# Down projections: loads of borrowed tiles and stored sums issued by GpSimd's queue instead of SyncE's

## The chip, the cores and the metric

The kernel runs on one core of one Trainium2 chip. The metric is the device time of one execution in microseconds (us). The engines are named as in the profile: PE (TensorE, with PEld for its weight loads), DVE (VectorE), ACT (ScalarE), POOL (GpSimd) and SP (SyncE). SPq and POOLq are the instruction queues of SP and POOL, which here issue DMA transfers.

## What is computed

A decoder trunk of two layers over 256 tokens of width 2048, all in float32. The part that the change touches is the gated feed-forward block at the end of each layer:

```python
def conv_ffn(h, w_up, cw, cb, w_down):
    S = h.shape[1]
    a = h @ w_up
    ap = jnp.pad(a, ((0, 0), (CONV_W - 1, 0), (0, 0)))
    c = sum(ap[:, k:k + S] * cw[k] for k in range(CONV_W)) + cb
    gate, val = c[..., :D_FF], c[..., D_FF:]
    return (jax.nn.silu(gate) * val) @ w_down
```

`w_up` is 2048 x 11264 and `w_down` 5632 x 2048 in each layer. The rest (token mixing, attention over memory and over the sequence, norms) is unchanged.

## The kernel before

Every float32 weight is split on the chip into a high and a low part of a reduced format (ACT writes the high part `whi`, DVE the low part `wlo`), and PE makes three products for each float32 product. The raw weights stream from memory into tiles named `raw`, of which there are four; `whi` has four tiles and `wlo` five.

`ffn` cuts the hidden width into three parts of 4, 4 and 3 groups of 512 columns (`FF_GROUPS`). For each part it makes the up projection of all groups (through `gemm_fm`), and then two down phases (`down_phase`, called with `col` 0 and 1024), one for each half of the 2048 output columns. A down phase goes over 8 (or 6) pairs of 128-row blocks of `w_down`, in an order written out in `FF_FAST`. A pair has two rows of blocks, each 128 x 1024 (512 KB).

- A pair that is not "fast" is split as it is (`plain_pair`) and takes 24 matmuls.
- A "fast" pair is multiplied by seven products in place of eight, which need sums of its blocks (`fast_pair`). Some sums are made while the up projection runs (`early_sums`, tiles `sums` and `xs`). Others were made still earlier, written to memory by POOL (`stored_sums`, line 800, tensors `stored`), and are loaded back in the down phase into `xs` tiles or a `staged` tile. The rest are made on the spot by DVE (`late_sums`, line 815).

Most rows land in `raw` tiles. Every third pair (the fifth and eighth of a first phase, the third and sixth of a second) lands in the two tiles `gate`, borrowed from the up projection, where they hold the silu gates. So a load into `gate` waits until DVE has read the last gate (line 1009), and later until the pair three places back has been split.

All these loads are issued at one line, 877, by SP's queue. `behind` ties each to the one before it on the same engine, so that SP issues them in the written order, and one that must wait for its tile holds up all behind it:

```python
load = lambda o, a: self.behind(self.nc.sync.dma_start(out=o, in_=a))
row = lambda i, c: load(raws[i][:, :c], dn[(2 * k + i) * P : (2 * k + i + 1) * P, col : col + c])
```

POOL's own queue has little to do: it issues the stores of the sums during the up projections, two loads at the seam between the layers (line 471, `kT` and `mv` out of `keptkv`), and makes some vector work in the mixers. In the last part of the last layer SP also issues four loads of the final gain (`gb`, line 1606) between the rows.

Of the kernel before, what the change touches and what calls it, by code (L numbers as in the profile page):

```python
# [16 lines left out]
P = 128  # L17
# [75 lines left out]
class Kernel:  # L93
# [747 lines left out]
    def down_phase(self, dn, col, order, fast, lhs, rhs, pool, fp, between, evict, finish, late=0, late_gains=None, hooks={}, sums={}, stored={}):  # L841
        mm = self.nc.tensor.matmul
        names = ("m1", "m5", "m6", "m7"), ("e00", "e01", "e10", "e11")
        acc = {n: self.psum() for group in (names[::-1] if fast else names[1:]) for n in group}
        left, right = slice(0, 512), slice(512, 1024)
        todo = {n: 0 for n in acc}
        for k in order:
            for n in ("m1", "m5", "m6", "m7", "e00", "e01", "e10") if k in fast else names[1]:
                todo[n] += 1 if k in fast else 2
        total = dict(todo)  # L850

        def three(n, x, w, out=None, ends=None):
            (xh, xl), (wh, wl) = x, w
            start, stop = (todo[n] == total[n], todo[n] == 1) if ends is None else ends
            todo[n] -= 1
            o = acc[n] if out is None else out
            mm(o, xh, wh, start=start, stop=False)  # L857
            mm(o, xh, wl, start=False, stop=False)  # L858
            mm(o, xl, wh, start=False, stop=stop)  # L859

        def plain(k, ws, tb, half, **kw):
            cols = (left, right)[half]
            for i, (wh, wl) in enumerate(ws):
                three(f"e{tb}{half}", lhs(2 * k + i, tb), (wh[:, cols], wl[:, cols]), **kw)

        kept = []
        last_fast = [k for k in order if k in fast][-1:]
        for n, k in enumerate(order):
            raws = []
            for i in range(2):  # L870
                if n % 3 == (2 if col else 1) and n > 1:
                    raw = self.tmp(fp, [P, 1024], "gate", 2)
                else:
                    raw = self.wp.tile([P, 1024], F32, tag="raw", name=self.uid("raw"), bufs=4)
                raws.append(raw)
            kept_sums = stored.get((k, col // 1024))
            load = lambda o, a: self.behind(self.nc.sync.dma_start(out=o, in_=a))
            row = lambda i, c: load(raws[i][:, :c], dn[(2 * k + i) * P : (2 * k + i + 1) * P, col : col + c])
            blocks = sums.get(k)
            if kept_sums is None:  # L880
                row(0, 1024 if blocks is None else 512)
                row(1, 1024)
            else:
                home = FF_STAGED[len(order) // 2].get((k, col // 1024))
                if home is not None:
                    tile = self.tokens.staged[:, home].rearrange("p m c -> p (m c)")
                    blocks = [tile[:, i * 1024 : (i + 1) * 1024] for i in range(2)]
                else:
                    blocks = [self.tmp(pool, [P, 1024], "xs", 2) for _ in range(2)]
                row(1, 1024)  # L890
                for i in (1, 0):
                    load(blocks[i], kept_sums[:, i])
                row(0, 512)
            if k in fast and blocks is None:
                blocks = self.late_sums(raws, pool)
            if late_gains is not None and 2 <= n:
                late_gains(n - 2)
            if k in fast:
                names7 = "e00", "e01", "e10", "m6", "m5", "m7", "m1"
                for name, q, w in zip(names7, (1, 6, 2, 5, 4, 3, 0), self.fast_pair(raws, blocks)):  # L900
                    three(name, rhs(k, q), w)
                if k in last_fast:
                    between([acc[m] for m in names[0]])
            else:
                ws = self.plain_pair(raws)
                if n < len(order) - late:
                    for tb in range(2):
                        for half in range(2):
                            plain(k, ws, tb, half)
                else:  # L910
                    kept.append((k, ws))
            for f in hooks.get(n, ()):
                f()
        if not late:
            for tb in range(2):
                for half in range(2):
                    evict(tb, half, acc[f"e{tb}{half}"])
            return
        ET = mybir.EngineType
        with self.tc.manual_schedule(engines={ET.PE, ET.DVE, ET.Activation}):  # L920
            for half in range(2):
                for k, ws in kept:
                    plain(k, ws, 0, half)
                evict(0, half, acc[f"e0{half}"])
            for k, ws in kept:
                plain(k, ws, 1, 0)
            evict(1, 0, acc["e10"], meanwhile=lambda: finish(0))
            for k, ws in kept[:-1]:
                plain(k, ws, 1, 1)
            k, ws = kept[-1]  # L930
            e, rest = acc["e11"], self.psum()
            for i, (wh, wl) in enumerate(ws):
                three("e11", lhs(2 * k + i, 1), (wh[:, 512:768], wl[:, 512:768]), out=e[:, :256], ends=(False, i == 1))
            evict(1, 1, e, 0)
            for i, (wh, wl) in enumerate(ws):
                three("e11", lhs(2 * k + i, 1), (wh[:, 768:], wl[:, 768:]), out=rest[:, 256:], ends=(i == 0, i == 1))
            evict(1, 1, rest, 1)
            finish(1)
# [506 lines left out]
class Tokens:  # L1445
# [46 lines left out]
    def between(self, accs):  # L1492
        for i, acc in enumerate(accs):
            self.nc.scalar.activation(self.staged[:, self.ph, i, :], acc, AF.Copy)
        self.waiting.append(self.ph)
# [26 lines left out]
    def finish(self, tb):  # L1522
        pass
# [5 lines left out]
class Inner(Tokens):  # L1529
# [27 lines left out]
    def evict(self, tb, half, acc):  # L1557
        j, o = self.added(tb, half, acc)
        if self.last:
            junk = self.quarters()[:, :512]  # L1560
            self.nc.scalar.activation(junk, o, AF.Square, accum_out=self.sums[:, tb, j : j + 1])
# [118 lines left out]
```

## Time and profile before

| | |
|---|---|
| median of three runs | 2019.14 us (2019.09 to 2020.36) |
| profiled execution, its own time | 2020.28 us |
| profiled execution, its span | 2018.6 us |
| PE busy | 2006.7 us (99%) |
| DVE busy | 1688.2 us (84%) |
| ACT busy | 1189.6 us (59%) |
| POOL busy | 141.4 us (7%) |
| moved by DMA | 488.45 MB, 242 GB/s over the span |

The span runs from the first to the last instruction of the profiled execution. An engine's busy time counts neither the waits nor the instructions that only issue a transfer on SP. The clock granted to PE is full in all slices.

### The profile page before, as it was taken

The numbers are of one execution on the slowest core, as the hardware profiler recorded it, in microseconds if no ns is written. First come the engines' busy times: TensorE is split into PE (matmuls) and PEld (weight loads), VectorE is DVE, ScalarE is ACT, GpSimd is POOL, SyncE is SP. The second block draws the span as 40 slices with busy tenths as digits, with TensorE's granted clock in tenths as the row PEclk, the third lists the DMA queues.
The fourth block names the chain that finished last, engine by engine and source line by source line (L and its number), as shares of the span: only waits on it lengthen the run. The fifth ranks groups of instructions, "written<-read, shape, count | busy, mean of one in ns | idle before, by whom it ended". The sixth has DMA issues, their size and how long they took to land.

```text
span 2018.6 us, 38495 instructions
## 1 busy us (share of the span) xinstructions
PE 2006.7 (99%) x15086; PEld 1903.3 (94%) x15086; DVE 1688.2 (84%) x2551; ACT 1189.6 (59%) x1691; POOL 141.4 (7%) x225
## 2 busy tenths in 40 slices
PE   9999999999999999999999999999999999999998
PEld 8989999999989999899989999999988999889996
DVE  6876867888898888899888887788889898898887
ACT  6754744555665556655566675455566455675565
POOL 0100013100000000000003142400000000000000
PEclk9999999999999999999999999999999999999999
DMA  8787787898578885888676635798868887578854
GB/s 256 236 234 214 241 264 256 222 319 276 188 285 281 266 246 169 302 285 264 213 244 209 203 114 202 234 252 293 262 207 286 276 301 239 198 277 251 257 187 172
DMA packets 272203, 488.45 MB, mean 242 GB/s; under 512 B 78030, under 2 KB 85524, under 8 KB 272020
## 3 DMA queue, kind: packets, MB, share of 16 engines
q1 hardware_dynamic: 263764, 456.08, 70.3%
q0 software_dynamic: 8064, 29.36, 4.0%
q8 instruction: 118, 1.93, 0.4%
q14 instruction: 65, 0.53, 0.1%
q10 hardware_dynamic: 192, 0.54, 0.1%
HBM read 450.79 MB, written 30.41 MB: 238 GB/s over the span
## 4 chain that ended last, share of the span: by engine, by line
PE 97%; DVE 1%; DMA 1%; ACT 1%; issue 0%; SPq 0%; ACTq 0%; DVEq 0%
PE ps L177 22%; PE ps L178 22%; PE ps L180 22%; PE ps L858 7%; PE ps L859 7%; PE ps L857 7%; PE ps L209 2%; PE ps L210 2%; PE ps L211 2%; PE ps L560 1%; DMA raw<-in_w_ffn_down 1%; DVE wlo L746 0%; PE ps L640 0%; PE ps L425 0%; PE ps L638 0%; PE ps L639 0%
## 5 line engine op out<-in xcount | busy, mean ns | idle before, releaser
L138 ACT ACTIVATE whi<-raw 128x1024 fp32r<-128x1024 f32 x484 | 513.5, 1062 | 518.8 <-PE ps L178 385.2
L177 PE MATMUL ps<-xhl,whi 128*128 128x256 f32 x3264 | 763.5, 277 | 0.0
L178 PE MATMUL ps<-xhl,whi 128*128 128x256 f32 x3264 | 761.7, 276 | 0.0
L139 DVE TENSOR_TENSOR wlo<-raw,whi 128x1024 fp32r<-128x1024 f32 x484 | 596.8, 1237 | 176.9 <-ACT whi L138 173.6
L177 PEld LDWEIGHTS ps<-xhl,whi 128*128 128x128 f32 x3264 | 612.8, 188 | 0.4
L178 PEld LDWEIGHTS ps<-xhl,whi 128*128 128x128 f32 x3264 | 612.8, 188 | 0.4
L180 PE MATMUL ps<-xhl,wlo 128*128 128x256 f32 x3264 | 438.4, 276 | 0.0
L180 PEld LDWEIGHTS ps<-xhl,wlo 128*128 128x128 f32 x3264 | 401.2, 188 | 0.0
L746 DVE TENSOR_TENSOR wlo<-raw,whi 128x1024 fp32r<-128x1024 f32 x94 | 114.0, 1221 | 33.3 <-ACT whi L745 32.2
L858 PE MATMUL ps<-wlo,h 128*128 128x512 f32 x354 | 137.1, 388 | 0.1
L745 ACT ACTIVATE whi<-raw 128x1024 fp32r<-128x1024 f32 x94 | 98.6, 1054 | 50.7 <-PE ps L178 36.4
L800 POOL DMA_DIRECT2D stored<-xs x52 | 28.2, 543 | 1372.3 <-DVE xs L762 804.6
L177 PE MATMUL ps<-mainhl,whi 128*128 128x256 f32 x512 | 119.6, 277 | 0.0
L178 PE MATMUL ps<-mainhl,whi 128*128 128x256 f32 x512 | 119.4, 276 | 0.0
L859 PE MATMUL ps<-whi,h 128*128 128x512 f32 (+1 forms) x306 | 118.4, 388 | 0.0
L975 ACT ACTIVATE c<-a,cT 128x256 f32<-128x256 f32 x176 | 99.5, 592 | 26.8 <-DVE a L257 25.9
L857 PE MATMUL ps<-whi,h 128*128 128x512 f32 x354 | 107.6, 388 | 0.6 <-ACT whi L745 0.6
L178 PEld LDWEIGHTS ps<-mainhl,whi 128*128 128x128 f32 x512 | 96.0, 188 | 0.0
L177 PEld LDWEIGHTS ps<-mainhl,whi 128*128 128x128 f32 x512 | 95.9, 188 | 0.0
L144 DVE SCALAR_TENSOR_TENSOR wlo<-raw,gT,whi 128x512 fp32r<-128x512 f32 x96 | 70.8, 776 | 17.3 <-ACT whi L143 17.0
L143 ACT ACTIVATE whi<-raw,gT 128x512 fp32r<-128x512 f32 x96 | 63.5, 715 | 33.2 <-DMA raw<-in_w_mem_kv 13.9
L257 DVE TENSOR_TENSOR a<-ps,rbc 128x256 f32<-128x256 f32 x176 | 69.6, 418 | 15.5 <-PE ps L180 15.5
(395 smaller groups left out, 3174.9 us busy)
## 6 DMA issues: line engine op xcount, KB each, us to landing
raw<-in_w_ffn_up SPq DMA_DIRECT2D x352, 512.0 KB, 4.8
raw<-in_w_ffn_down SPq DMA_DIRECT2D x102, 512.0 KB, 7.0
xs<-in_w_ffn_down SPq DMA_DIRECT2D x64, 512.0 KB, 6.1
raw<-in_w_out SPq DMA_DIRECT2D x64, 512.0 KB, 4.8
raw<-in_w_in_a SPq DMA_DIRECT2D x56, 512.0 KB, 4.9
stored<-xs POOLq DMA_DIRECT2D x52, 512.0 KB, 5.1
raw<-in_w_mem_kv SPq DMA_DIRECT2D x31, 512.0 KB, 4.8
gate<-in_w_ffn_down SPq DMA_DIRECT2D x30, 512.0 KB, 7.0
```

Of the source, the lines that this page charges most:

```text
L138: nc.scalar.activation(hi[:, :n], raw[:, :n], AF.Copy)
L139: nc.vector.tensor_tensor(lo[:, :n], raw[:, :n], hi[:, :n].bitcast(F32), ALU.subtract)
L144: nc.vector.scalar_tensor_tensor(lo[:, s], raw[:, s], gains[k], hi[:, s].bitcast(F32), ALU.mult, ALU.subtract)
L177: mm(acc[:, :S], wh, x[:, :S], start=first, stop=False)
L178: mm(acc[:, :S], wh, x[:, S:], start=False, stop=False)
L180: mm(acc[:, :S], wl, x[:, :S], start=False, stop=last)
L745: self.behind(self.nc.scalar.activation(hi, w, AF.Copy))
L746: self.behind(self.nc.vector.tensor_tensor(lo, w, hi.bitcast(F32), ALU.subtract))
L857: mm(o, xh, wh, start=start, stop=False)
L858: mm(o, xh, wl, start=False, stop=False)
L859: mm(o, xl, wh, start=False, stop=stop)
L975: nc.scalar.activation(c, a, AF.Identity, scale=w(2), bias=w(3))
```

## The change

Rows that land in `gate` tiles, and all loads of stored sums, are issued by POOL's queue; rows into `raw` tiles stay on SP's. Since `behind` keeps one chain for each engine, the two queues keep the written order each for itself, and neither waits for the other.

```diff
-            raws = []
+            raws, away = [], n % 3 == (2 if col else 1) and n > 1
             for i in range(2):
-                if n % 3 == (2 if col else 1) and n > 1:
+                if away:
                     raw = self.tmp(fp, [P, 1024], "gate", 2)
                 else:
                     raw = self.wp.tile([P, 1024], F32, tag="raw", name=self.uid("raw"), bufs=4)
                 raws.append(raw)
             kept_sums = stored.get((k, col // 1024))
-            load = lambda o, a: self.behind(self.nc.sync.dma_start(out=o, in_=a))
-            row = lambda i, c: load(raws[i][:, :c], dn[(2 * k + i) * P : (2 * k + i + 1) * P, col : col + c])
+            load = lambda o, a, queue=self.nc.gpsimd: self.behind(queue.dma_start(out=o, in_=a))
+            source = self.nc.gpsimd if away else self.nc.sync
+            row = lambda i, c: load(raws[i][:, :c], dn[(2 * k + i) * P : (2 * k + i + 1) * P, col : col + c], source)
             blocks = sums.get(k)
```

Over the whole program 96 loads leave SP's queue for POOL's: 44 rows into `gate`, 28 loads into `staged` and 24 into `xs`. 132 rows into `raw` stay.

On SP, in the first down phase of the second part of layer 0 (the numbers after names tell tiles apart; `raw_9681` is the second row of the fourth pair, and the raw tiles 9758 and 9759 are the two rows of the sixth pair, 9799 and 9800 of the seventh):

```order
 L877 DMA raw_9681<-in_w_ffn_down 128x1024
-L877 DMA gate_9719<-in_w_ffn_down 128x512
-L877 DMA gate_9720<-in_w_ffn_down 128x1024
 L877 DMA raw_9759<-in_w_ffn_down 128x1024
-L877 DMA staged_9560<-stored_5302 128x1024 x2
 L877 DMA raw_9758<-in_w_ffn_down 128x512
 L877 DMA raw_9800<-in_w_ffn_down 128x1024
-L877 DMA xs_9802<-stored_5694 128x1024
-L877 DMA xs_9801<-stored_5694 128x1024
 L877 DMA raw_9799<-in_w_ffn_down 128x512
```

Six loads leave the place between the rows of the fourth, sixth and seventh pair, and those rows now follow one another.

On SP, in the first down phase of the last part of layer 1 (`raw_23816` and `raw_23817` are rows of the sixth pair, `raw_23888` and `raw_23889` those of the first pair of the second phase):

```order
-L1606 DMA gb<-in_g_final 128x512
-L877 DMA gate_23776<-in_w_ffn_down 128x512
-L877 DMA gate_23777<-in_w_ffn_down 128x1024
-L1606 DMA gb<-in_g_final 128x512
+L1607 DMA gb<-in_g_final 128x512 x2
 L877 DMA raw_23817<-in_w_ffn_down 128x1024
-L877 DMA staged_23614<-stored_22852 128x1024 x2
 L877 DMA raw_23816<-in_w_ffn_down 128x512
-L1606 DMA gb<-in_g_final 128x512
+L1607 DMA gb<-in_g_final 128x512
 L877 DMA raw_23888<-in_w_ffn_down 128x1024
 L877 DMA raw_23889<-in_w_ffn_down 128x1024
```

The two gate rows and the two staged loads are gone from between them; the `gb` loads are the same and only show another line number.

On POOL, at the end of layer 0 (`kT` and `mv` are the two loads of the seam):

```order
+L877 DMA gate_12128<-in_w_ffn_down 128x512
+L877 DMA gate_12129<-in_w_ffn_down 128x1024
+L877 DMA staged_11969<-stored_10744 128x1024 x2
+L877 DMA gate_12329<-in_w_ffn_down 128x1024
+L877 DMA gate_12330<-in_w_ffn_down 128x1024
 L471 DMA kT_12510<-keptkv 128x1024
+L877 DMA gate_12457<-in_w_ffn_down 128x1024
+L877 DMA gate_12458<-in_w_ffn_down 128x1024
 L471 DMA mv_12511<-keptkv 128x1024
```

Here the last two gate rows of layer 0 come to stand behind the load of `kT` and ahead of that of `mv`.

## Rows read from the trace of the kernel before

**Rows 1.** The page, its head and the busy time of PE.

```profile
span 2018.6 us, 38495 instructions
PE 2006.7 (99%) x15086; PEld 1903.3 (94%) x15086; DVE 1688.2 (84%) x2551; ACT 1189.6 (59%) x1691; POOL 141.4 (7%) x225
```

**Rows 2.** The waits of PE at line 857: total us, times, longest us.

```profile
PE ps L857 <- ACT staged L1494: 0.8, 1, 0.8
PE ps L857 <- ACT whi L745: 0.6, 1, 0.6
```

**Rows 3.** Windows: length, busy us of PE, PEld, DVE, ACT, POOL; PEclk, DMA, GB/s.

```profile
787.00:791.00 4.00, 4.00 (x19) 3.30 (x19) 4.00 (x9) 2.77 (x4) 0.00 (x0) 1.00 0.06 22
807.00:811.00 4.00, 3.55 (x16) 2.62 (x14) 2.52 (x3) 1.92 (x3) 0.00 (x0) 1.00 1.00 330
2005.00:2018.60 13.60, 4.72 (x27) 3.97 (x25) 6.72 (x21) 5.02 (x13) 0.00 (x0) 0.79 0.40 155
```

**Rows 4.** Timeline of SP, 783 to 806: start us, us, merged instructions.

```profile
783.81 9.25 SPq L877 DMA_DIRECT2D gate<-in_w_ffn_down  x2
793.46 0.33 SPq L877 DMA_DIRECT2D raw<-in_w_ffn_down  x1
799.30 1.43 SPq L877 DMA_DIRECT2D staged<-stored  x2
800.77 0.91 SPq L877 DMA_DIRECT2D raw<-in_w_ffn_down  x2
```

**Rows 5.** Timeline of DVE in the same stretch.

```profile
788.56 1.21 DVE L746 TENSOR_TENSOR wlo<-raw,whi 128x1024 fp32r<-128x1024 f32 x1
794.98 0.69 DVE L746 TENSOR_TENSOR hhx<-raw,hhx 128x512 fp32r<-128x512 f32 x1
795.58 1.22 DVE L746 TENSOR_TENSOR wlo<-raw,whi 128x1024 fp32r<-128x1024 f32 x1
```

**Rows 6.** Timeline of ACT, 803 to 811: idle time before, and its releaser, in brackets.

```profile
804.69 1.06 ACT L745 ACTIVATE whi<-staged 128x1024 fp32r<-128x1024 f32 x1 [0.22 <-DMA staged<-stored]
...
808.36 0.63 ACT L745 ACTIVATE hhx<-raw 128x512 fp32r<-128x512 f32 x1 [1.03 <-DMA raw<-in_w_ffn_down]
810.05 1.06 ACT L745 ACTIVATE whi<-raw 128x1024 fp32r<-128x1024 f32 x1 [1.05 <-DMA raw<-in_w_ffn_down]
```

**Rows 7.** Timeline of SP, 1957 to 1966.

```profile
1962.60 0.80 SPq L877 DMA_DIRECT2D staged<-stored  x2
1963.45 0.42 SPq L877 DMA_DIRECT2D raw<-in_w_ffn_down  x1
1963.92 0.43 SPq L1606 DMA_DIRECT2D gb<-in_g_final  x1
1964.39 1.45 SPq L877 DMA_DIRECT2D raw<-in_w_ffn_down  x2
```

**Rows 8.** Timelines of DVE and, the last row, of ACT, 1958 to 1975.

```profile
1958.29 0.68 DVE L746 TENSOR_TENSOR hhx<-raw,hhx 128x512 fp32r<-128x512 f32 x1
...
1962.70 0.68 DVE L746 TENSOR_TENSOR hhx<-raw,hhx 128x512 fp32r<-128x512 f32 x1
...
1974.87 1.06 ACT L745 ACTIVATE whi<-raw 128x1024 fp32r<-128x1024 f32 x1 [1.71 <-DMA raw<-in_w_ffn_down]
```

**Rows 9.** Issue time on each queue, ns min/median/max, over the whole span.

```profile
L800 POOL DMA_DIRECT2D stored<-xs x52: 531/531/602, 196.1 to 1883.0; - x52
L877 SPq DMA_DIRECT2D xs<-stored x24: 326/326/327, 548.9 to 1790.8; - x24
```

**Rows 10.** DMA issues: median us from issue to landing.

```profile
raw<-in_w_uk SPq DMA_DIRECT2D x6, 512.0 KB, 3.6
kT<-keptkv POOLq DMA_DIRECT2D x1, 512.0 KB, 5.6
```

**Rows 11.** Timelines of POOL and, the last row, of SP at the end of layer 0.

```profile
1029.64 0.55 POOL L471 DMA_DIRECT2D kT<-keptkv  x1 [65.53 <-ACT whi L745]
1033.20 2.60 SPq L877 DMA_DIRECT2D gate<-in_w_ffn_down  x2
```

## The prediction

> **What bounds the kernel now.** I read the page first. PE is busy 2006.7 of 2018.6 us, so 11.9 us are all that it is ever idle [rows 1]. Next the windows: in the last 13.6 us PE is busy for 4.72, so 8.9 of the 11.9 lie at the tail, where the last results are evicted and written out [rows 3]. The list of PE's waits has just two in the down phases, one of 0.8 and one of 0.6 us [rows 2]; what is left lies in other stages, at the very start above all. What one row of the page can't say, these views say together: everything in the down phases but 1.4 us is hidden behind PE. The change issues transfers elsewhere; it takes no matmul away. So it can give back about 1.4 us, and it can lose as much as it makes PE wait.
>
> **Where the 0.6 us come from.** The first down phase of the second part of layer 0. SP issues a first gate row at 783.81; the second must wait for DVE's last reading of a gate, and the two take until 793.06. Then one raw row goes out at 793.46, and the staged loads behind it wait until 799.30 for their tile, which the early sums still fill [rows 4]. Meanwhile the DMA engines are nearly unused (a share of 0.06 from 787 to 791), and afterwards everything goes out in one burst, in which they are full: a share of 1.00 from 807 to 811, at 330 GB/s [rows 3]. ACT then waits 1.03 us for one raw row and 1.05 for the next [rows 6], and PE waits 0.6 for what ACT makes of the second.
>
> How much earlier could the raw rows go, if nothing held them but their tiles? The row at 793.46 lands in the tile that DVE reads from 788.56 to 789.77. The two at 800.77 land in tiles read until 795.67 and 796.80 [rows 4, 5]. They would go out 3.7, 5.1 and some 4.4 us earlier (the last of them at about 801.2). That moves 512 + 256 + 512 KB, 1.31 MB, out of the burst into time in which the engines have room. At 330 GB/s this is 4.0 us of the burst. The row for which PE waited then has from 796.8 to 810.05 to land, 13 us. I count the whole 0.6 us as returned.
>
> **Where the 0.8 us come from.** The last part of layer 1. A raw row goes out at 1963.45, then a gain load, then two raw rows from 1964.39 on, the second at about 1965.2; all stand behind the staged loads of 1962.60 [rows 7]. ACT waits 1.71 us for that last row, until 1974.87 [rows 8]; its next work is the eviction for which PE waits 0.8. So ACT could have started at 1974.1 without harm: the row must land 0.8 us sooner. In the changed order the row of 1963.45 needs the tile that DVE leaves at 1958.97, and the first of the two the tile left at 1963.38 [rows 8]. The 256 KB row and the 256 KB gain load thus leave the burst (0.52 MB, 1.6 us at 330 GB/s), and the row in question goes out at about 1963.8, 1.4 us sooner. Either would do for 0.8. I count it as returned too, though the staged loads now share the engines with it from the other queue, where they went ahead before.
>
> **What the change adds.** 96 issues on POOL at 0.531 us, where SP took 0.326 [rows 9]: 51 us more work on an engine that is busy for 141 and has no other work in the down phases but the two loads at the end of layer 0. SP is rid of 96 issues; nobody waits for SP's time itself. As both queues keep the written order, no load stands behind one that it didn't stand behind before, with two exceptions on POOL. One is the stores of sums (line 800), which are issued in the up projections and are over when a down phase starts. The other is the end of layer 0, where the last two gate rows come to stand behind the load of `kT`. That went out at 1029.64, and the first of the two rows had its tile at 1033.20 [rows 11]: 3.6 us of cover, and if it were gone the rows would be late by as much as `kT` is. The load of `mv`, now behind them, is not read before the next layer's attention over memory. ACT's order changes in four places, where one `whi` out of `xs` now stands ahead of the eviction of a fast product; it is one ACT step of 1.06 us [rows 6], and the bank it frees is not wanted in the first pair of the next phase, which is plain and has 24 matmuls. I cost it at nothing.
>
> **The price that the trace lacks** is a load of `w_down` or of sums issued by POOL in such a burst, and issues of POOL right behind one another. From below: it starts 0.2 us later than SP's, the difference of the issues. From above: `kT`, issued by POOL, landed after 5.6 us, and the best loads of the same size by SP after 3.6 [rows 10], so 2.0 us. I take the lower end, since in the burst the transfer waits for bandwidth and not for its start, and both kinds of transfer share the engines. A gain from the earlier start of these loads is excluded: they wait for their tiles as before.
>
> POOL's 52 issues of before took 531 ns (median and minimum) and 602 at most, while DVE is busy for 84% of the span [rows 1, 9], so I count the new ones at 0.531 us too. A rule of the Trainium skill speaks against that (SBUF — State Buffer, "SBUF: two separate sides"): the descriptors of a transfer issued by GpSimd are written by GpSimd's cores, and VectorE locks these out during some of its instructions. By the rows the sum gets 0 from this, by the rule the loss of the third rival; so far the trace doesn't show the rule at work.
>
> **The sum.** -0.6 - 0.8 = -1.4 us, and 0 for the rest. For the profiled execution that is 2020.28 - 1.4 = 2018.9; the median of the runs shown lies 1.14 below that execution's own time, so the forecast is 2019.14 - 1.4 = 2017.7 us.
>
> **The rivals.**
> 1. *Nothing moves.* The burst is as many bytes as before, and the engines are full in it [rows 3]. If the staged loads, now in a queue of their own, take as much from the raw rows as these gain by starting early, PE's two waits stay: 2019.1 us. For it speaks that the second of the two waits rests on 1.4 us only; against it, that the engines idle before both bursts. The Trainium skill's page DMA: Bandwidth & Descriptors says under "Issuing engines are not separate DMA queues" that a second issuing engine saves no more than issuing time; what is removed here is a wait in an order, of which it doesn't speak.
> 2. *POOL's loads land later than SP's did.* One mechanism: the two staged loads of a first phase, then the two into `xs`. At 804.69 ACT already waits 0.22 us for a staged load [rows 6], so there is no lead to eat up in this phase, and 2.0 us of lateness would be 2.0 us of PE. The other three parts of four groups have the same order of loads, and PE waits in none of them [rows 2], so they have some lead; each pays between 0 and 2.0. The time is between 2019.1 + 2.0 = 2021.1 and 2019.1 + 8.0 = 2027.1, around 2024. It decides as soon as the lateness is more than the 0.6 us that PE gets back there.
> 3. *VectorE holds POOL's issues up.* If each issue had to wait for one DVE step of 1.22 us [rows 5], the run of eight loads in the first phase of a four-group part (two staged, two `xs`, a gate, two staged, a gate) would end 8 x 1.22 = 9.8 us later; with no lead to cover it, the four such phases lose 4 x 9.8 = 39 us: 2058 us. Rows 9 speak against it.
>
> That the change doesn't do what it says is excluded by the orders shown above.
>
> **How the numbers follow.** 0.2% is 4.0 us, about what a measurement of this kernel can tell from no change. My forecast gets 0.60, the first rival 0.31, the second 0.06, the third 0.02, and 0.01 is left for something that I don't see. Faster by over 4.0 us would need almost three times what PE waits in the down phases: 0.01. The forecast and the first rival lie within 0.2%: 0.91. The second, over most of its span, and the third are slower: 0.08. The range takes in the forecast with all runs a little lower than the median shown (2016.9), the first rival with a run as high as 2020.36, and the low end of the second, 2021.1, which I round to 2021.2.
>
> **What would show it.** In the profile after: POOL with 51 us more busy time and 96 more issues of some 0.53 us; in SP's timeline the raw rows after 789, 796 and 797 instead of at 793.46 and 800.77; a DMA share well above 0.06 between 787 and 799; ACT without the waits of 1.03, 1.05 and 1.71 us for raw rows; PE's list of waits without the two of line 857. I am wrong if PE waits for `whi` made from `staged`, `xs` or `gate` (the second rival), if POOL's issues last 1 us and more (the third), or if both waits of line 857 are still there (the first).

## The result and the profile after

The changed kernel takes 2027.76 us (median of 5 runs, 2025.38 to 2028.15); the kernel before, on the same chip, 2019.25 us (2019.09 to 2020.89). The ratio is 1.0037, 95% interval [1.0026, 1.0048]: slower by 8.5 us, where 1.4 us of gain were forecast. The change does what it says, and the two old waits are gone; larger ones have come.

The page of the kernel after, its head, PE's and POOL's busy time, the DMA queues and the chain by engine ([rows 1] before):

```profile
span 2026.1 us, 38556 instructions
PE 2009.4 (99%) x15086; PEld 1902.2 (94%) x15086; DVE 1688.3 (83%) x2551; ACT 1190.5 (59%) x1691; POOL 193.3 (10%) x321
...
q1 hardware_dynamic: 249940, 409.41, 63.4%
q0 software_dynamic: 20992, 76.03, 10.9%
...
PE 93%; DMA 3%; DVE 2%; ACT 1%; issue 1%; POOL 0%; SPq 0%; ACTq 0%; DVEq 0%; POOLq 0%
PE ps L177 22%; PE ps L178 22%; PE ps L180 22%; PE ps L857 6%; PE ps L858 5%; PE ps L859 5%; DMA staged<-stored 3%; PE ps L209 2%; PE ps L210 2%; PE ps L211 2%; PE ps L560 1%; DVE wlo L746 1%; ACT whi L745 1%; PE ps L640 0%; PE ps L638 0%
```

q1 is the queue that SP feeds, q0 the one that POOL feeds. Nothing but the queue of 96 loads has changed, yet loads of stored sums now hold 3% of the chain that ended last.

PE's waits at line 857 after ([rows 2] before), and below ACT's waits for `staged` loads at line 745, after and before: total us, times, longest us.

```profile
PE ps L857 <- ACT whi L745: 6.3, 6, 2.4
```

```profile
ACT whi L745 <- DMA staged<-stored: 20.7, 16, 3.9
```

```profile
ACT whi L745 <- DMA staged<-stored: 1.3, 4, 0.5
```

PE waited 1.4 us in two places before. After the change it waits 6.3, in six other places, each time for a `whi` that ACT makes from a late load, and ACT's waits for `staged` grew from 1.3 to 20.7 us. PE's busy time is also 2.7 us longer for the same 15086 matmuls: a matmul that starts after a stall counts a little longer (below, two count 0.74 us at 565.42; the same two took 0.62 before, at 564.64).

**Where it is lost.** The length of each part's down phases, from the start of the first matmul of lines 857 to 860 to the end of the last, read from PE's timeline (us):

| kernel | parts of layer 0 | parts of layer 1 | sum |
|---|---|---|---|
| before | 79.75, 80.66, 63.64 | 79.75, 79.75, 64.44 | 447.99 |
| after | 81.02, 82.54, 63.64 | 81.55, 81.17, 65.92 | 455.84 |

The sum grows by 7.85 us, inside the interval of the ratio (5 to 10 us). The four parts of four groups lose 1.27, 1.88, 1.80 and 1.42; the last part loses 1.48. What lies outside the down parts, the same in all kernels of this document, takes between 1569.7 and 1572.2 us in their traces (span less sum), without an order that follows from the edits. So a single time scatters by some 2 us for reasons outside the change, and the sums below tell the versions apart better than the times do.

**One place in full.** The first part of layer 0 starts its down phases at 528.12 us before and 528.14 after, so that times compare directly. Timelines of SP and ACT before (start, us, merged instructions; in brackets idle time and its releaser):

```profile
552.51 0.92 SPq L877 DMA_DIRECT2D staged<-stored  x2
...
554.01 2.12 SPq L877 DMA_DIRECT2D raw<-in_w_ffn_down  x2
...
560.21 1.05 ACT L745 ACTIVATE whi<-staged 128x1024 fp32r<-128x1024 f32 x1
561.44 1.06 ACT L745 ACTIVATE whi<-staged 128x1024 fp32r<-128x1024 f32 x1 [0.18 <-PE ps L859]
```

and of POOL, SP, ACT and PE after:

```profile
552.52 0.54 POOL L877 DMA_DIRECT2D staged<-stored  x1
553.35 0.55 POOL L877 DMA_DIRECT2D staged<-stored  x1 [0.30 <-issue]
...
552.93 0.33 SPq L877 DMA_DIRECT2D raw<-in_w_ffn_down  x1
555.82 1.81 SPq L877 DMA_DIRECT2D raw<-in_w_ffn_down  x2
...
561.70 1.06 ACT L745 ACTIVATE whi<-staged 128x1024 fp32r<-128x1024 f32 x1 [1.37 <-DMA staged<-stored]
564.31 1.06 ACT L745 ACTIVATE whi<-staged 128x1024 fp32r<-128x1024 f32 x1 [1.55 <-DMA staged<-stored]
...
565.42 0.74 PE L857 MATMUL ps<-whi,hmv 128*128 128x512 f32 x2 [0.60 <-ACT whi L745]
```

These are the staged loads of the eighth pair, and the rows of the second phase's first pairs. All are issued at nearly the same times in both kernels (one raw row 1.1 us earlier). Before, ACT never waited for the two staged loads; after, it waits until they land, 9.2 and 11.0 us after their issue, so the second is at least 2.9 us later. Now what the queues moved in the stretch from 558 to 566 us (packets, MB, share of 16 engines), first before, then after:

```profile
q1 hardware_dynamic: 959, 3.22, 101.7%
```

```profile
q0 software_dynamic: 417, 1.48, 51.1%
q1 hardware_dynamic: 419, 1.49, 49.7%
```

The engines are full in both. Before, one queue had them whole, and in its written order the staged loads stand ahead of the next phase's rows. After, the two queues get half each, almost to the packet. The rows that PE wants only in the next phase take half of the bandwidth from the loads that it wants now.

In the last part POOL issues the staged loads of the sixth pair at 1969.27; SP has by then issued a raw row and a gain load, and at 1966.53 a row of the next phase, all of which stood behind the staged loads before [rows 7]. ACT and PE after:

```profile
1978.29 1.06 ACT L745 ACTIVATE whi<-staged 128x1024 fp32r<-128x1024 f32 x1 [3.94 <-DMA staged<-stored]
...
1979.40 0.50 PE L857 MATMUL ps<-whi,h 128*128 128x512 f32 x1 [2.37 <-ACT whi L745]
```

A load takes 9.0 us here, and PE loses 2.37, where it lost 0.8 for another reason before [rows 2]. The even sharing of the eighth pair isn't what the packets show here. From 1970.50 to 1978.00:

```profile
q0 software_dynamic: 365, 1.35, 58.1%
q1 hardware_dynamic: 208, 0.71, 32.9%
```

POOL's queue moved 1.35 MB, more than its two staged loads hold (1.05 MB), and the first of them landed only at 1978.29. So part of the gate row that POOL issued behind them, at 1971.21, moved before the first was in.

### The profile page after: what moved, and what is told of

Its sections match the earlier page's. It is cut to its first block, busy times and chain, and to the rows that moved or that the text cites. A ratio compares the mean times of both kernels' runs of the same rounds, so it can differ in the third digit from the quotient of the medians.

```text
span 2026.1 us, 38556 instructions
## 1 busy us (share of the span) xinstructions
PE 2009.4 (99%) x15086; PEld 1902.2 (94%) x15086; DVE 1688.3 (83%) x2551; ACT 1190.5 (59%) x1691; POOL 193.3 (10%) x321
## 4 chain that ended last, share of the span: by engine, by line
PE 93%; DMA 3%; DVE 2%; ACT 1%; issue 1%; POOL 0%; SPq 0%; ACTq 0%; DVEq 0%; POOLq 0%
PE ps L177 22%; PE ps L178 22%; PE ps L180 22%; PE ps L857 6%; PE ps L858 5%; PE ps L859 5%; DMA staged<-stored 3%; PE ps L209 2%; PE ps L210 2%; PE ps L211 2%; PE ps L560 1%; DVE wlo L746 1%; ACT whi L745 1%; PE ps L640 0%; PE ps L638 0%
```

## The experiments

Three theories stood at the start. Theory 1: two queues share the engines, so the written order of urgency is lost between them. Theory 2: POOL's queue is slow by itself. Theory 3: DVE holds up POOL's issues.

### Transfers alone: b1_bench

Six stages, one after the other, of 512 KB rows of `w_down` into free tiles: eight by SP (tiles `spt`), eight by POOL (`plt`), both together, and the three again beside 16 additions of DVE.

```diff
+        stage(True, False, 0)
+        stage(False, True, 0)
+        stage(True, True, 0)
+        stage(True, False, 16)
+        stage(False, True, 16)
+        stage(True, True, 16)
```

> A kernel that leaves the decoder out: it only loads rows of w_down, eight transfers of 512 KB (4.19 MB) on SP's queue, then eight on POOL's, then eight on each at once; then the same three stages while DVE runs additions of 128x1024 with two inputs; its output is zeros. Theory 1 (the queues are alike, and the loss comes from sharing the engines, so that urgent loads no longer go first): SP alone and POOL alone take the same time, 10.5 to 12 us each at 350 to 400 GB/s; both at once take twice that, half each. Theory 2 (POOL's queue moves its transfers slower by itself): POOL alone takes 15 us or more, under 280 GB/s, where SP takes 10.5 to 12. Theory 3 (DVE holds POOL's issues up): POOL alone is like SP, and only with DVE's additions beside it do its issues grow from 0.54 us to 1 us and more, and its eight loads take 15 us or more.

Packets by queue in three stretches: POOL alone, 1.7 us from its first issue; both together, 4.4 us from POOL's first issue; both together, later.

```profile
q0 software_dynamic: 18, 0.07, 21.9%
...
q1 hardware_dynamic: 293, 1.09, 84.7%
q0 software_dynamic: 3, 0.01, 0.7%
...
q1 hardware_dynamic: 337, 1.25, 51.4%
q0 software_dynamic: 338, 1.25, 51.1%
```

POOL's timeline, alone without and beside the additions:

```profile
20.76 4.30 POOL L38 DMA_DIRECT2D plt<-in_w_ffn_down  x8 [20.31 <-DVE plt L33]
...
85.41 4.16 POOL L38 DMA_DIRECT2D plt<-in_w_ffn_down  x8 [44.13 <-DVE plt L33]
```

Alone, the median load lands after 7.4 us by SP and 8.0 by POOL; together, after 10.3 and 15.7. Two things make POOL's later in the mix. Its first packets move only some 4 us after the issue, where alone they have begun within 1.7; and from then on the queues have half each (337 and 338 packets). Eight issues take 4.30 us, and 4.16 with DVE at work; with both queues and DVE at work, one issue comes 0.54 us late, for one of the additions by the trace. Each set alone took longer than theory 1 said (10.5 to 12 us): 13.6 us by SP and 14.4 by POOL, from the first issue until DVE reads the last tile, and so a little less than theory 2's 15. By either queue, from the second load on, they land one after the other, some 1.3 us apart (1.5 once). So POOL's queue is nearly as fast as SP's when it is alone (against theory 2), and DVE hardly holds up its issues (against theory 3).

### Parts of the change: e1_gates_only, e2_sums_only, e3_all_pool

Against the changed kernel, e1, e2 and e3 in this order:

```diff
-            load = lambda o, a, queue=self.nc.gpsimd: self.behind(queue.dma_start(out=o, in_=a))
+            load = lambda o, a, queue=self.nc.sync: self.behind(queue.dma_start(out=o, in_=a))
```

```diff
-            source = self.nc.gpsimd if away else self.nc.sync
+            source = self.nc.sync
```

```diff
-            source = self.nc.gpsimd if away else self.nc.sync
+            source = self.nc.gpsimd
```

Only the gate rows by POOL:

> Only the 44 rows into gate tiles go to POOL; staged and xs loads are back on SP, in the written order with the raw rows. Theory 1 (sharing): the staged loads go ahead of the next phase's rows again, but share with the gate rows; PE waits 0 to 0.5 us in each of the six down parts, so +0 to +2 us against before. Theory 2 (POOL slow): the gate rows land late, but they have the longest lead; +0 to +3 us. Under both the greater part of the 8.5 us must be gone if it hangs on the stored sums.

Only the stored sums:

> Only the 52 loads of stored sums go to POOL; gate rows are back on SP. Theory 1 (sharing): fewer bytes on POOL's queue, so each staged load gets its half of the engines for less; +2 to +5 us against before. Theory 2 (POOL slow): the staged loads land as late as in the change; +5 to +9 us, with PE's waits for whi made of staged tiles in the same places, and the wait of 2.4 us in the last part kept.

All 228 loads of the down phases, in the old order:

> All 228 loads of the down phases go to POOL's queue, in the written order of before; SP has none. There is one order again and no sharing between queues, but SP's advantage is gone too. Theory 1 (sharing): within 2 us of before (2019). Theory 2 (POOL slow): slower than the change, since the raw rows are slow now too: 2035 us and more, with PE waiting in all down parts.

| kernel | median us | ratio to before, interval | down parts, sum |
|---|---|---|---|
| before (24 runs) | 2019.38 | | 447.99 |
| e1_gates_only | 2023.85 | 1.0022 [1.0013, 1.0032] | 455.31 |
| e2_sums_only | 2024.31 | 1.0025 [1.0015, 1.0035] | 451.51 |
| e3_all_pool | 2017.92 | 0.9991 [0.9982, 1.0001] | 446.39 |

(Sums are those of the one profiled execution; those of e1 and e3 were their longest runs.) Each half of the change loses more than half of the whole, 4.5 and 4.9 us: either one is enough to break the order. For e1_gates_only I had expected 3 us at most under both theories; the loss doesn't hang on the stored sums alone. In e2_sums_only the last part has no wait at line 857 (63.56 us, against 65.92 after the change). With every load on POOL nothing is lost, so theory 2 falls. PE's waits in e3_all_pool have none of line 857 left; its whole list of waits is

```profile
PE ps L527 <- DVE ones L307: 1.1, 1, 1.1
PE ps L349 <- DMA graw<-in_g_mem: 0.5, 1, 0.5
PE ps L640 <- DVE pT L266: 0.2, 1, 0.2
```

e1_gates_only shows that gate rows can be intruders too. There the staged loads stay on SP, ahead of the raw rows as before, and in the last part it is gate rows of the second phase that POOL issues early, at 1967.44 and 1971.44, ahead of or among raw rows that SP issues from 1967.03 on. POOL and ACT in e1_gates_only, and then PE's wait:

```profile
1967.44 0.54 POOL L877 DMA_DIRECT2D gate<-in_w_ffn_down  x1 [7.37 <-DVE wlo L746]
1971.44 0.54 POOL L877 DMA_DIRECT2D gate<-in_w_ffn_down  x1 [3.47 <-DVE hhx L746]
...
1979.84 1.06 ACT L745 ACTIVATE whi<-raw 128x1024 fp32r<-128x1024 f32 x1 [2.96 <-DMA raw<-in_w_ffn_down]
```

```profile
PE ps L857 <- ACT staged L1495: 3.2, 1, 3.2
```

The old wait of 0.8 us for that eviction, behind the same raw rows, has become 3.2.

### Which rows intrude, and does it matter whose queue: e5_next_behind, e6_next_alone, e7_exchanged

The rival left was that POOL's transfers alone lose beside SP's, as their late start in the mix might suggest. 24 rows, those into raw tiles of the first two pairs of each second phase, are the suspects.

Against the changed kernel, e5 has them on POOL too, behind the staged loads:

```diff
-            source = self.nc.gpsimd if away else self.nc.sync
+            source = self.nc.gpsimd if away or (col and n < 2) else self.nc.sync
```

e6 is the kernel before with only these rows on POOL:

```diff
-            load = lambda o, a, queue=self.nc.gpsimd: self.behind(queue.dma_start(out=o, in_=a))
-            source = self.nc.gpsimd if away else self.nc.sync
+            load = lambda o, a, queue=self.nc.sync: self.behind(queue.dma_start(out=o, in_=a))
+            source = self.nc.gpsimd if col and n < 2 else self.nc.sync
```

and e7 is the change with the queues exchanged:

```diff
-            load = lambda o, a, queue=self.nc.gpsimd: self.behind(queue.dma_start(out=o, in_=a))
-            source = self.nc.gpsimd if away else self.nc.sync
+            load = lambda o, a, queue=self.nc.sync: self.behind(queue.dma_start(out=o, in_=a))
+            source = self.nc.sync if away else self.nc.gpsimd
```

> The change, and also the four rows into raw tiles of the first two pairs of each second phase on POOL's queue, where they stand behind the staged loads of the eighth pair again. Theory 1: these 24 rows are what the staged loads shared the engines with, so the waits of PE for the eighth pair's staged tiles (0.6, 0.7 and 0.9, 0.9, 0.8 us) and the 2.4 us in the last part go or fall under 0.2 us each; down parts 447 to 449 us, time 2017.5 to 2020.5. Rival (any load on POOL beside a stream on SP starts late and lands late, whichever rows SP carries): the waits for staged tiles stay at half their size or more, 2023 to 2028.

> The kernel before, with the same 24 rows alone on POOL's queue; all gate rows and stored sums stay on SP's in their old order. Theory 1 (shared engines, lost order, alike for both queues): the staged loads, though issued by SP, land some us later than before and PE waits for them at the eighth pair again, 0.3 to 0.9 us a time and 1 to 3 us in the last part: 2021 to 2027 us. Rival (only POOL's transfers lose beside SP's): the staged loads land as before, PE has no wait for them; what may come late are the 24 rows themselves, which have some us of lead: 2018 to 2020.5.

> The split of the change with the queues exchanged: gate rows and stored sums stay on SP's queue, rows into raw tiles go to POOL's. Theory 1 (alike for both queues): the same loss as the change, 2024 to 2030 us, with PE waiting for whi out of staged at the eighth pair. Rival (only POOL's transfers lose): no waits for staged tiles; waits for raw rows in their place, or none: under 2022 us, or over 2030 if the raw rows come too late throughout.

| kernel | median us | ratio to before, interval | down parts, sum |
|---|---|---|---|
| before (21 runs) | 2019.09 | | 447.99 |
| e5_next_behind | 2019.82 | 1.0004 [0.9995, 1.0012] | 447.72 |
| e6_next_alone | 2026.38 | 1.0036 [1.0023, 1.0049] | 453.51 |
| e7_exchanged | 2027.38 | 1.0042 [1.0028, 1.0056] | 454.26 |

**e5.** With the 24 rows behind the staged loads again the loss is gone, though 120 loads are POOL's: one wait of PE of line 857 is left, and from 558 to 566 us one queue has the engines whole again.

```profile
PE ps L857 <- ACT whi L745: 0.3, 1, 0.3
```

```profile
q0 software_dynamic: 858, 3.10, 101.1%
```

**e6.** The reverse: 24 rows alone, moved into a queue of their own, bring back most of the loss. ACT waits for staged loads that SP issued, in the old order and at the old time. The queues from 558 to 566 us, and in the last part from 1972 to 1975; PE's waits; and ACT at the eighth pair of layer 0's second part:

```profile
q0 software_dynamic: 455, 1.65, 52.2%
q1 hardware_dynamic: 490, 1.52, 49.7%
...
q1 hardware_dynamic: 303, 0.96, 95.0%
q0 software_dynamic: 7, 0.03, 2.8%
```

```profile
PE ps L857 <- ACT whi L745: 3.6, 3, 1.5
```

```profile
818.92 1.06 ACT L745 ACTIVATE whi<-staged 128x1024 fp32r<-128x1024 f32 x1 [1.59 <-DMA staged<-stored]
821.49 1.06 ACT L745 ACTIVATE whi<-staged 128x1024 fp32r<-128x1024 f32 x1 [1.51 <-DMA staged<-stored]
```

The 1 to 3 us that I expected in e6's last part didn't come: it has no wait (63.30 us, against 65.92 after the change). POOL issues one row there at 1967.38, ahead of the staged loads (SP, 1969.59), and it is mostly in by 1970 (0.41 MB). The next, issued at 1970.66, starts late, as in b1_bench: from 1972 to 1975 SP's queue moves 0.96 MB and POOL's 0.03. At the eighth pair of layer 0's first part it is the same. POOL issues a first row at 553.49, and until 557.25 one queue alone moves:

```profile
q1 hardware_dynamic: 480, 1.48, 102.9%
```

Here theory 1 needs an amendment. Where both queues had begun, they shared evenly; but a load that came upon engines that the other queue kept full began to move only some 4 us after its issue. (The row of 1967.38 began after 1.2, as SP's queue ran dry.) It isn't POOL's alone. In e5_next_behind SP issues a row at 568.16, beside a full POOL queue, and until 571.50 one queue alone moves again, POOL's:

```profile
q0 software_dynamic: 342, 1.23, 98.0%
```

In the last part of e6 the lag was enough to hold the intruder off, at the eighth pairs not.

**e7.** With SP carrying the urgent loads and POOL the raw rows the loss is the same within the intervals, and ACT waits 15.0 us for `staged`:

```profile
ACT whi L745 <- DMA staged<-stored: 15.0, 16, 1.6
...
PE ps L857 <- ACT staged L1495: 1.4, 2, 0.8
...
PE ps L857 <- ACT whi L745: 0.8, 3, 0.3
```

PE's waits are spread otherwise here: the longest two are behind late raw rows, which are POOL's in this kernel. So the rival falls too. In the parts of four groups it matters little which engine issues (4.9 us longer in sum than before, against 6.4 after the change); what costs is that rows of lesser urgency stand in another queue than the loads that they used to follow. In the last part it does matter: 65.92 us after the change, 64.42 with SP carrying the urgent loads. A late start isn't the reason: after the change POOL's queue begins to move within 1.3 us of the issue at 1969.27. Nor do the next phase's raw rows suffice: in e2_sums_only SP issues them at the same times in the part, beside POOL's staged loads, and PE doesn't wait. What e2 lacks is POOL's early gate row of 1971.21, which stands *behind* the staged loads in their own queue. Theory 1 doesn't say how a row behind them can hold them back, so the largest single wait, 2.37 us, is only in part explained; it goes in e5, where the 24 rows stand in POOL's queue too and that gate row behind them.

### What a better order is worth: e4_sp_by_readiness, e8_pool_by_readiness, e9_all_pool_again

The wait that the change removes can also be removed within one queue, by issuing the loads of the fifth to seventh pair of a first phase in the order in which their tiles come free. The core of the edit (`row(n, i)` issues row i of pair n unless it is out already); e8 has `gpsimd` in place of `sync`, and e9 is e3_all_pool once more.

```diff
+            if col == 0 and n == 4:
+                place(5)
+                for m, i in ((4, 0), (5, 1), (4, 1), (5, 0)):
+                    row(m, i)
...
+                row(n, 1)
+                if col == 0 and n == 5:
+                    if len(order) > 6:
+                        row(6, 1)
...
+                row(n, 0)
+                if col == 0 and n == 5 and len(order) > 6:
+                    row(6, 0)
```

> All loads on SP's queue as before, but in a first down phase those of the fifth to seventh pair are issued in the order in which their tiles come free (a gate row, the sixth pair's second row, the other gate row, the sixth pair's first row, the seventh pair's second row, the staged loads, ...). Theory 1 (what costs is that two queues share the engines and lose the written order; the head-of-line wait itself is worth what PE waits at line 857): PE's wait of 0.6 us in the second part and of 0.8 us in the last part go, no new wait comes, the down parts sum to 446.4 to 447 us as with all loads on POOL, time 2017.4 to 2018.4. Rival (the gain of all loads on POOL came from POOL's queue itself and not from the order): both waits stay, 2019 to 2020.

> The loads in the order of e4_sp_by_readiness, all issued by POOL. Theory 1 (one queue, order of urgency kept): no wait of PE for staged, xs or gate; as all loads on POOL in the old order have left PE no wait in the down parts (446.4 us in sum), nothing is left to win: down parts 446.3 to 447, time 2017.3 to 2018.7, within 0.5 us of e9_all_pool_again. Rival (POOL's one queue and the order by readiness each give a part of the gain, so they add): under 2017.

> The kernel of e3_all_pool once more, for a closer interval: if PE's two waits of line 857 are worth what its trace lacks of them, 1.4 to 1.6 us below the kernel before, ratio 0.9992 to 0.9994, so 2017.3 to 2018.3; if the first measurement was scatter, a ratio of 0.9996 to 1.0003.

| kernel | median us | ratio to before, interval | down parts, sum |
|---|---|---|---|
| e4_sp_by_readiness | 2018.90 | 0.9998 [0.9989, 1.0006] | 446.89 |
| e8_pool_by_readiness | 2017.82 | 0.9991 [0.9982, 1.0] | 446.35 |
| e9_all_pool_again | 2017.95 | 0.9991 [0.9982, 1.0] | 446.06 |

(Before: 2019.09 beside e4, 2019.55 beside e8 and e9.) In all three PE has no wait of line 857 left, and the down parts are shorter by 1.1 to 1.9 us. (e9 and e3 are one kernel, with sums 0.33 apart.) So the size of the gain that I forecast was about right, and it needs one queue, not two. With e4 the time doesn't show it: 0.2 us, outside the 2017.4 to 2018.4 that I expected; its sum is that of its longest run. With one queue of POOL's it is 1.6 to 1.7 us here and 1.5 in e3_all_pool; the intervals reach 1.0 (1.0001 there). The two gains don't add, as theory 1 expected: nothing is left to win. Of what was tried, all loads on POOL is the best version by the median.

## Why the prediction was wrong

**What held.** PE is the bound, and the change can lose as much as it makes PE wait. The 96 loads moved, at 537 to 540 ns for 531 forecast; POOL's busy time rose by 51.9 us for 51. Line 877 after, ns min/median/max:

```profile
L877 POOL DMA_DIRECT2D gate<-in_w_ffn_down x44: 537/540/562, 499.5 to 1998.2; - x44
L877 POOL DMA_DIRECT2D staged<-stored x28: 537/537/547, 545.9 to 1969.8; - x28
L877 POOL DMA_DIRECT2D xs<-stored x24: 537/537/554, 549.2 to 1797.5; - x24
```

No issue is stretched, so the third rival fell, and the rule of the Trainium skill beside it (SBUF — State Buffer, "SBUF: two separate sides") isn't seen at work here. The raw rows of the second part went out when the prediction said: at 791.10, 796.99 and some 798.1 in a trace in which that part starts 1.29 us later, so 789.8, 795.7 and 796.8 for 789.77, 795.67 and 796.80 forecast. ACT's waits of 1.03 and 1.05 us there [rows 6], and PE's of 0.6 behind them [rows 2], are gone. In size the steps -0.6 and -0.8 are borne out by e4_sp_by_readiness, where these rows go out early in one queue and nothing else is spoiled: neither wait is left, and the down parts are 1.10 us shorter. One sign was ill chosen: the DMA share from 787 to 799 is 0.37 after, but it was 0.29 before; the 0.06 was that of 787 to 791 alone.

**The step that failed** is the price that the trace lacks: what a load pays when POOL issues it in the burst. The prediction took its lower end, 0.2 us, "since in the burst the transfer waits for bandwidth and not for its start, and both kinds of transfer share the engines", and put it at 0 in the sum. Sharing the engines is the price: PE's waits at line 857 went from 1.4 to 6.3 us, and the down parts grew by 7.85. In one queue at the eighth pair, what stood behind the staged loads cost them nothing that PE saw; beside a second full queue they had half of the engines. An earlier sentence, "no load stands behind one that it didn't stand behind before", is true and beside the point: 24 rows that stood *behind* the urgent loads now stand beside them. I looked at what each load must wait for and not at what it had been protected from. Of the last part I did write that the staged loads "now share the engines with it from the other queue, where they went ahead before", and drew no price from it.

**The upper end was wrong too.** It came from landing times of single loads, 2.0 us [rows 10], which say nothing of a burst. The right bound is worked out from the bytes that a load must now let pass: three rows of 512 KB and one of 256 KB of the next phase, 1.8 MB, at the 330 GB/s of the burst [rows 3] up to 5.6 us (an estimate). The second staged load of the eighth pair was at least 2.9 us late. From its issue to its landing, 553.35 to 564.31, SP's queue moved 1.28 MB of such rows, which at the 336 GB/s of that stretch is 3.8 us.

**The second rival** came nearest to the case that came (POOL's loads land late, PE waits for `whi` from `staged`), with a chance of 0.06 and a time of 2021.1 to 2027.1; measured 2027.76. That its upper end lies so close is luck, for its place and its cause were others. It named the staged loads of the sixth pair and those into `xs` in the parts of four groups. Five of the six waits stand at the eighth pair, and one in the last part, which it left out: all six at the last pair of a first phase, beside which the rows of the next phase go out. Nor is it mainly a lateness of POOL's own, as e6 and e7 show.

**The page cited beside the first rival** (the Trainium skill, DMA: Bandwidth & Descriptors, "Issuing engines are not separate DMA queues") also says that transfers started by different engines "interleave with each other". The trace agrees: 417 and 419 packets in 8 us. I used only its other half, that a second issuing engine saves no more than issuing time.

## What to carry to other kernels

When loads keep the DMA engines full, a single queue in the order of need is a priority list; moving some of it into a second queue gave less urgent rows about half of the bandwidth here. Price such a split, from above, by the bytes that stood behind each urgent load and now stand beside it, divided by the burst's rate, and set that against the lead that the load has. If a load holds up others that are ready, change the order within the queue, or move the whole list, before splitting it.

## What the runs showed that I had not expected

- Two full queues shared the engines evenly, almost to the packet: 337 and 338 in 6 us in b1_bench, 417 and 419 in 8 us in the kernel after. In the last part after the change they didn't (365 and 208 in 7.5 us), and why is open.
- A load whose engines were already busy for the other queue started late: 3 packets after 4.4 us for POOL in b1_bench, against 18 after 1.7 us alone, and none after 3.3 us for SP in e5_next_behind. In the last part of e6_next_alone this lag kept two staged loads from harm.
- With all loads on POOL the old wait of 0.6 us in layer 0's second part went, although the order is the old one and the two rows that ACT waited for were issued only 0.14 us earlier relative to the start of the part (528 to 784 us into the span the two traces are 1.87 us apart). The first burst ran faster. Windows of that burst in e3_all_pool, and the same stretch before (length, busy us of PE, PEld, DVE, ACT, POOL; PEclk, DMA share, GB/s):

```profile
804.87:810.87 6.00, 6.00 (x28) 4.98 (x27) 6.00 (x7) 4.37 (x6) 4.08 (x8) 1.00 1.02 384
```

```profile
803.00:809.00 6.00, 6.00 (x28) 4.98 (x27) 5.83 (x6) 4.23 (x5) 0.00 (x0) 1.00 0.98 283
```

The engines count as full in both, but move 384 GB/s for POOL (367 in e9_all_pool_again, the same kernel) and 283 for SP. In b1_bench, with rows of `w_down` alone, the two queues are nearly equal, so it isn't the queue by itself. What it is stays open; no run tried that burst's mix of rows and sums by itself.
